# A macaron layer with neighbourhood and dilated attention: the layout in DRAM of queries, keys and values, and the order in which they are read back

## The chip, the core and the metric

The kernel runs on one core of one Trainium2 chip. The time is the device time of one execution in microseconds (us); of the kernel before there are three runs, of which the median counts. The engines are called as in the profile: PE is TensorE (matmuls; PEld its weight loads), DVE VectorE, ACT ScalarE, POOL GpSimd, SP SyncE. SP computes nothing here; it only issues transfers. POOL computes a little and issues transfers too. All of an engine's instructions, its transfers among them, go out in the order in which they stand: one that waits holds all behind it.

## What is computed

One layer on x of 1024 tokens by 1024 numbers, in fp32. Each of its three parts normalises its input and its output (RMSNorm) and adds the result to x:

```python
h = swiglu(rmsnorm(x, g1), w_gate, w_up, w_down);  x = x + 0.5 * rmsnorm(h, g2)
h = rmsnorm(x, mix_pre_g)
q, k, v = split(h @ w_qkv)                         # 16 heads of 64
o_na  = neighbourhood_attention(q[:8], k[:8], v[:8], rel_bias)
o_dil = dilated_mixture_attention(q[8:], k[8:], v[8:], t5_bias)
mixed = concat(rmsnorm(o_na), rmsnorm(o_dil)) @ w_out;  x = x + rmsnorm(mixed, g3)
h = swiglu(rmsnorm(x, g4), ...);                   x = x + 0.5 * rmsnorm(h, g5)
```

The tokens form a grid of 16 rows by 64 columns. In neighbourhood attention a token sees 8 rows by 16 columns about it, with a learned bias. In dilated attention it sees three windows (every token, every 4th, every 16th) with a bias by distance, and the three results are merged by their softmax denominators.

## The kernel before, in words

**Precision.** Each fp32 operand is split into a high part (fp32r) and a low part, the remainder. A product of two matrices is three matmuls (lines 262 to 264).

**Stages.** First the FFN, then a stage for values, queries and keys (the normalised rows and the weights are cut in quarters, and seven products of sums of quarters take the place of eight), then attention, the output projection and the second FFN. Values, queries, keys and bias tables go through DRAM: a stage writes them, and attention reads them per head in another layout.

**What is written.** The values are kept per token as a row of 4 x 130 numbers: 4 pairs of heads, each with 2 x 64 numbers and two ones, which give the softmax sums. `c.v[0]` holds those of neighbourhood, `c.v[1]` those of dilated attention, in the order of tokens. They are written by POOL, 128 tokens to a transfer, at line 1427 (`vearly`, half of the neighbourhood values) and line 1448 (`vrows`, the others). `QKPairs.put` (lines 817 to 845) writes queries and keys of a pair of heads, half of the tokens at a time: ACT casts the high part (line 834), DVE makes the low part (line 835), and POOL writes each part with a transfer of its own into `c.qk[p][kind]`, of shape [2 parts, 128, 1024]. Line 840 writes neighbourhood queries, which are permuted into strips; line 843 dilated keys, permuted by token modulo 4; line 845 the rest in plain order. The tile `e` that holds both parts has three buffers while queries and keys are made; ACT waits at line 829 or 834 if none is free.

**What is read.** The heads come in pairs: 4 to 7 (dilated) first, then 0 to 3 (neighbourhood). `load_head` (line 1334) asks for a head's data, and for a pair's values ahead of its first head:
- its stack (`load_stack`, lines 848 to 858), by POOL. The tile `st` has 128 partitions. Slot 0 holds the query: its high part on partitions 0 to 63, its low part on 64 to 127. Slots 1 and 2 hold the high and the low part of the key, on both halves alike. One matmul with slot 1 and one with slot 2 (lines 981 and 1093) then give all four products of parts. The stack is read with four transfers, a query and a key transfer for each half. The tile is fp32r, its source fp32, so the transfers cast. There are two buffers, and for every third dilated head one in another pool.
- the values. `dil_values` (line 900) loads those of pair 4 when its first head is loaded, and those of pairs 5 to 7 in one piece with pair 5: `va` for the near windows in twelve transfers of 32 partitions, `vb` for the far ones in four of 128. `na_v` (line 1058) loads a neighbourhood pair's `vs` in 16 transfers of 8 partitions. All are issued by SP.
- its bias table, by SP: `DilPair.bias` (line 935, tile `g`, two transfers) or `na_bias` (line 1066, tile `nb`). POOL then copies or adds to the table (lines 863 and 1537) before DVE uses it.

The order in `load_head` is: stack, then values if the head is its pair's first, then the table. Each SP transfer also waits for the one issued eight before it.

**A head.** It is a row of units. Each unit makes scores (line 981 or 1093), takes the row maxima together with the bias (DVE, line 881), exponentials (ACT, line 886), transposes them (line 892), copies the result (line 897) and multiplies with the values (line 993 or 1106); the steps of several units overlap, and the scores run ahead of the value products by four units. A dilated head has 8 units: `part` 1 (far windows, `vb`) and `part` 0 (near windows, `va`); only the very first head begins with `part` 0. A neighbourhood head has 8 units too. When the dilated heads have been merged, matmuls of the output projection are spread among the units that are left, at an even rate. The order of PE, DVE and ACT in this stage is that in which the code is written; SP and POOL are ordered by the scheduling layer, by dependence and readiness.

Of the kernel before, what the change touches and what calls it, by code (L numbers as in the profile page):

```python
# [19 lines left out]
P, T = 128, 512  # L20
# [776 lines left out]
class QKPairs:  # L797
# [19 lines left out]
    def put(self, b, kind, h, x):  # L817
# [18 lines left out]
        d = c.qk[p][kind]  # L836
        for j in range(2):
            if strip:
                dst = d[j].rearrange("p (s r c) -> p s (r c)", s=8, r=16)[:, :, h * 64:h * 64 + 64]
                nc.gpsimd.dma_start(dst, e[:, j].bitcast(F32).rearrange("p (s x) -> p s x", s=8))  # L840
            elif kind and p >= NP:
                dst = d[j].rearrange("p (c h t) -> p h c t", c=4, h=2)[:, h]
                nc.gpsimd.dma_start(dst, parts[j].bitcast(F32))
            else:
                nc.gpsimd.dma_start(d[j, :, h * T:(h + 1) * T], e[:, j].bitcast(F32))


def load_stack(c, p, hd, pool):

    nc = c.nc  # L850
    st = pool.tile([P, 3, SEQ], F32R, tag="st", name="st", bufs=2 if pool is c.stk else 1)
    rows = slice(hd * 64, hd * 64 + 64)
    q, k = c.qk[p]
    for u in range(2):
        dst = slice(u * 64, u * 64 + 64)
        nc.gpsimd.dma_start(st[dst, 0, :], q[u, rows, :])
        nc.gpsimd.dma_start(st[dst, 1:3, :], k[:, rows, :].rearrange("j p n -> p j n"))
    return st
# [41 lines left out]
def dil_values(c, pool, p, n):  # L900

    w, row = n * VW, 16 * VW
    va = pool.tile([P, 11, w], F32, tag="va", name="va", bufs=1)
    vb = pool.tile([P, 4, 2, w], F32, tag="vb", name="vb", bufs=1)
    v = c.v[1][:, (p - NP) * VW:(p - NP) * VW + w]
    for ci in range(4):
        to = va[ci * 32:ci * 32 + 32]
        for u0, m, t0 in ((0, 7, 16), (7, 2, 0), (9, 2, 192)):
            c.nc.sync.dma_start(to[:, u0:u0 + m], bass.AP(tensor=v.tensor, offset=v.offset + ci * 4 * VW + t0 * row,
                                                          ap=[[row, 32], [32 * row, m], [1, w]]))  # L910
    for ci in range(4):
        c.nc.sync.dma_start(vb[:, ci], v.rearrange("(j i c) f -> c i j f", j=2, c=4)[ci])
    return va, vb


class DilPair:
# [17 lines left out]

    def bias(self, hd, third):
        c, nc = self.c, self.c.nc
        g = (c.op if third else c.gp).tile([P, 3, 384], F32, tag="g", name="g", bufs=1 if third else 2)
        for i in range(2):
            nc.sync.dma_start(g[:, 2 - i], c.gab[i][2 * self.pi + hd, :, 127:511])
        return g  # L940
# [10 lines left out]
    def unit(self, hd, st, q, g, part, quad, un, po):  # L951
# [5 lines left out]
        def scores():  # L957
# [4 lines left out]
            for j in range(2):  # L962
# [8 lines left out]
                else:  # L971
# [5 lines left out]
                    ex = sj.rearrange("p (c u t) -> p u c t", c=4, u=2)  # L977
                    pj = pb[:, j].rearrange("p (u c t) -> p u c t", u=2, c=4)
# [79 lines left out]
def na_v(c, p):  # L1058
    vs = c.vp.tile([P, 8, VW], F32, tag="v" + "ab"[p % 2], name="vs")
    src = c.v[0][:, p * VW:(p + 1) * VW].rearrange("(r s c) f -> r c s f", r=16, s=8)  # L1060
    for r in range(16):
        c.nc.sync.dma_start(vs[r * 8:r * 8 + 8], src[r])
    return vs

# [106 lines left out]
def layer(tc, a, out):  # L1171
    nc = tc.nc
    c = Ctx(tc)
    with ExitStack() as ctx:
# [20 lines left out]
        c.qk = [[c.dr.tile([2, P, SEQ], F32, name=f"qk{p}_{k}") for k in range(2)] for p in range(8)]  # L1195
# [138 lines left out]
        def load_head():  # L1334
# [23 lines left out]
        with ExitStack() as order:  # L1358
# [64 lines left out]
            def vearly(p, t, ps):  # L1423
# [3 lines left out]
                nc.gpsimd.dma_start(vs1[t] if p == 0 else c.v[0][t * P:(t + 1) * P, :], v)  # L1427
# [18 lines left out]
            def vrows(t, h):  # L1446
                for g in range(t < 4, 2):
                    nc.gpsimd.dma_start(c.v[g][t * P:(t + 1) * P, :], h[:, g])
# [227 lines left out]
```

## Time and profile before

| | us |
|---|---|
| three runs, median (lowest, highest) | 1956.05 (1955.32, 1956.93) |
| the profiled execution, its own time | 1954.08 |
| its span in the trace | 1952.3 |
| TensorE busy in the span | 1867.3 |
| VectorE, ScalarE, GpSimd busy | 1313.9, 804.1, 325.4 |
| TensorE busy from 900 to 1000 us / 1000 to 1100 / 1100 to 1200 | 89.16 / 99.33 / 87.42 |

How to read the rows that follow. A row of a stretch gives its start and end, its length, then for each engine the busy us and, in brackets, the number of instructions; then the granted clock of TensorE (1.00 is full), the share of time in which the 16 DMA engines were busy, and GB/s. A row of the timeline gives start, length, engine, line, operation, output and inputs, how many are merged, and in square brackets the idle time before it and what ended it. A row of waits gives the waiting engine and line, what it waited for, the total in us, how often, and the longest. An engine named with a q (SPq) is its issuing side. "DMA st<-qk" is a transfer into tile `st` from tensor `qk`.

### The profile page before, as it was taken

To read this page: it belongs to the slowest core of one execution; us is meant where nothing else is said; L and a number is where in the kernel's file an instruction comes from. 1 tells how busy PE (TensorE), PEld (TensorE's weight loads), DVE (VectorE), ACT (ScalarE), POOL (GpSimd) and SP (SyncE) were. 2 spreads that over 40 slices of the span, in tenths; PEclk is the share of its full clock that TensorE was granted. 3 is DMA by queue.
4 is the path that set the end of the run, shared out by engine and by line. 5 is a ranking of instruction groups with operands and counts; after the bars stand their busy time and mean duration, and the time that the engine had idled before them with its cause. 6 is when DMAs were issued, how large, how long until landed. Compare 5 with 4: busy or idle time off the path is not lost.

```text
span 1952.3 us, 25216 instructions
## 1 busy us (share of the span) xinstructions
PE 1867.3 (96%) x9044; PEld 1559.5 (80%) x9044; DVE 1313.9 (67%) x2205; ACT 804.1 (41%) x1287; POOL 325.4 (17%) x536
## 2 busy tenths in 40 slices
PE   5999999999999989999899889998999999999997
PEld 4788888888888868778799887776888888888886
DVE  5778776765656766567456556676788777754557
ACT  4522333333534445233567655454222333344332
POOL 2101111111000123233443310121011111110000
PEclk8999999999999999999899989998999999999999
DMA  6555565546976667768997961574556665476663
GB/s 241 214 172 178 178 236 194 211 161 237 324 250 207 244 216 251 242 217 228 281 205 135 199 125 44 183 276 160 168 183 208 233 216 194 153 265 225 197 231 131
DMA packets 165246, 400.97 MB, mean 205 GB/s; under 512 B 18737, under 2 KB 35297, under 8 KB 165121
## 3 DMA queue, kind: packets, MB, share of 16 engines
q1 hardware_dynamic: 113616, 224.63, 36.4%
q0 software_dynamic: 50640, 172.64, 27.8%
q10 hardware_dynamic: 864, 2.10, 0.3%
q8 instruction: 71, 1.16, 0.2%
q14 instruction: 55, 0.44, 0.1%
HBM read 274.84 MB, written 129.50 MB: 207 GB/s over the span
## 4 chain that ended last, share of the span: by engine, by line
PE 78%; DMA 9%; DVE 6%; issue 5%; ACT 1%; POOL 1%; SPq 0%; DVEq 0%; POOLq 0%; ACTq 0%
PE mmp L264 16%; PE mmp L262 16%; PE mmp L263 16%; PE accp L263 7%; PE accp L264 7%; PE accp L262 7%; PE po L993 2%; PE ptp L892 2%; PE trp L170 1%; PE sp L981 1%; DMA vs<-v 1%; PE po L1106 1%; DMA g<-gab 1%; DMA x<-x 1%; DMA va<-v 1%
## 5 line engine op out<-in xcount | busy, mean ns | idle before, releaser
L262 PE MATMUL mmp<-x,whi 128*128 128x512 f32 (+1 forms) x1464 | 579.7, 396 | 7.6 <-ACT whi L355 3.6
L264 PE MATMUL mmp<-x,wlo 128*128 128x512 f32 (+1 forms) x1464 | 574.9, 393 | 1.0 <-DVE wlo L356 1.0
L263 PE MATMUL mmp<-x,whi 128*128 128x512 f32 (+1 forms) x1464 | 574.5, 392 | 0.6 <-DVE x L172 0.5
L262 PEld LDWEIGHTS mmp<-x,whi 128*128 128x128 f32 x1464 | 277.9, 190 | 67.5 <-ACT whi L355 4.2
L264 PEld LDWEIGHTS mmp<-x,wlo 128*128 128x128 f32 x1464 | 277.8, 190 | 62.2 <-DVE wlo L356 1.9
L263 PEld LDWEIGHTS mmp<-x,whi 128*128 128x128 f32 x1464 | 278.1, 190 | 59.8 <-DVE x L172 1.5
L613 DVE TENSOR_TENSOR pw<-praw,pw 128x1024 fp32r<-128x1024 f32 (+1 forms) x182 | 199.3, 1138 | 122.8 <-ACT pw L612 122.4
L612 ACT CAST pw<-praw 128x1024 fp32r<-128x1024 f32 (+1 forms) x182 | 169.5, 983 | 206.0 <-PE accp L264 167.7
L355 ACT CAST whi<-wraw 128x1024 fp32r<-128x1024 f32 x129 | 135.2, 1050 | 249.4 <-PE mmp L263 216.7
L262 PE MATMUL accp<-pw 128*128 128x512 f32 x600 | 234.4, 391 | 0.6 <-DVE hb L684 0.6
L264 PE MATMUL accp<-pw 128*128 128x512 f32 x600 | 233.5, 389 | 0.0
L263 PE MATMUL accp<-pw 128*128 128x512 f32 x600 | 233.4, 389 | 0.0
L356 DVE TENSOR_TENSOR wlo<-wraw,whi 128x1024 fp32r<-128x1024 f32 x129 | 157.6, 1225 | 24.9 <-ACT whi L355 24.8
L262 PEld LDWEIGHTS accp<-pw 128*128 128x128 f32 x600 | 112.6, 188 | 24.2 <-issue 1.0
L264 PEld LDWEIGHTS accp<-pw 128*128 128x128 f32 x600 | 112.6, 188 | 23.5
L263 PEld LDWEIGHTS accp<-pw 128*128 128x128 f32 x600 | 112.7, 188 | 23.3
L560 POOL DMA_DIRECT2D g<-sg x44 | 23.9, 542 | 472.3 <-DVE sg L553 285.6
L374 ACT COPY s<-mmp 128x512 f32<-128x512 f32 x52 | 30.5, 587 | 147.9 <-PE mmp L264 146.3
L518 DVE TENSOR_TENSOR c<-mmp,u 128x512 f32<-128x512 f32 x52 | 35.9, 691 | 82.5 <-PE mmp L264 82.2
L172 DVE TENSOR_TENSOR x<-trp,x 128x512 fp32r<-128x512 f32 x84 | 57.2, 687 | 35.0 <-ACT x L171 35.0
L355 ACT CAST whi<-traw 128x512 fp32r<-128x512 f32 x52 | 32.3, 621 | 116.9 <-PE mmp L263 58.4
L443 DVE TENSOR_TENSOR wraw<-wraw 128x1024 f32<-128x1024 f32 x52 | 63.6, 1224 | 23.6 <-DMA wraw<-in_wqk_dram 12.5
(230 smaller groups left out, 2739.2 us busy)
## 6 DMA issues: line engine op xcount, KB each, us to landing
praw<-g SPq DMA_DIRECT2D x70, 512.0 KB
wraw<-in_wg_dram SPq DMA_DIRECT2D x44, 512.0 KB
wraw<-in_wu_dram SPq DMA_DIRECT2D x44, 512.0 KB
tr<-in_wd_dram SPq DMA_DIRECT2D x44, 512.0 KB
g<-sg POOLq DMA_DIRECT2D x88, 256.0 KB, 3.9
ts<-tr POOLq DMA_DIRECT2D x22, 1024.0 KB, 4.7
praw<-ts SPq DMA_DIRECT2D x88, 256.0 KB
praw<-in_wd_dram SPq DMA_DIRECT2D x66, 256.0 KB
```

Of the source, the lines that this page charges most:

```text
L172: nc.vector.tensor_sub(lo, ps, hi.bitcast(F32))
L262: nc.tensor.matmul(out, ahi, bhi, start=start, stop=False, skip_group_check=go_on)
L263: nc.tensor.matmul(out, ahi, blo, start=False, stop=False, skip_group_check=go_on)
L264: nc.tensor.matmul(out, alo, bhi, start=False, stop=stop, skip_group_check=go_on)
L355: nc.scalar.copy(hi, raw)
L356: nc.vector.tensor_sub(lo, raw, hi.bitcast(F32))
L443: nc.vector.tensor_sub(r[:, 0:2], r[:, 1:3], r[:, 0:2])
L518: nc.vector.tensor_add(c21, d, u2)
L612: nc.scalar.copy(w[side][:, 0, :m], raw[:, :m])
L613: nc.vector.tensor_sub(w[side][:, 1, :m], raw[:, :m], w[side][:, 0, :m].bitcast(F32))
L892: c.nc.tensor.transpose(self.tps[:, j, :], self.probs[:, j * P:(j + 1) * P], c.ident)
L993: nc.tensor.matmul(po[0][:, un * 2 + j], u.pt[:, 2 * j + t, :], rhs, start=t == 0, stop=t == 1)
```

## The change

Six edits. PE, DVE and ACT keep their instructions and their order, save for the permutation in 5:

1. `c.qk` has the shape [128, 2 parts, 1024]: the parts of a row alternate. `put` writes both parts of plain rows with one transfer; permuted ones still take two.
2. `load_stack` reads the stack in two transfers over 128 partitions. High and low part of the query alternate by partition, and each partition gets both key parts of its row as one run of 8 KB. The destination is written as fp32, so nothing is cast.
3. The values in DRAM stand in the order of use: `put_values` writes them, with two transfers for every 128 tokens where there was one. `na_v` reads a pair's with one transfer, `dil_values` reads `va` with three transfers of 128 partitions.
4. `vb` is read with eight transfers (four residues, two halves) where there were four.
5. The exponentials of `part` 0 are written in another permutation, so that the keys agree with the new order of the values.
6. In `load_head` a head's table is asked for ahead of its pair's values; `dil_bias` is the former method `bias`.

```diff
@@ QKPairs.put
+        if not strip and not (kind and p >= NP):
+            nc.gpsimd.dma_start(d[:, :, h * T:(h + 1) * T], e.bitcast(F32))
+            return
         for j in range(2):
             if strip:
-                dst = d[j].rearrange("p (s r c) -> p s (r c)", s=8, r=16)[:, :, h * 64:h * 64 + 64]
+                dst = d[:, j].rearrange("p (s r c) -> p s (r c)", s=8, r=16)[:, :, h * 64:h * 64 + 64]
...
-            else:
-                nc.gpsimd.dma_start(d[j, :, h * T:(h + 1) * T], e[:, j].bitcast(F32))
@@ load_stack
-    rows = slice(hd * 64, hd * 64 + 64)
-    q, k = c.qk[p]
-    for u in range(2):
-        dst = slice(u * 64, u * 64 + 64)
-        nc.gpsimd.dma_start(st[dst, 0, :], q[u, rows, :])
-        nc.gpsimd.dma_start(st[dst, 1:3, :], k[:, rows, :].rearrange("j p n -> p j n"))
+    q, k = [bass.AP(tensor=x.tensor, offset=x.offset + hd * 64 * 2 * SEQ, ap=ap)
+            for x, ap in zip(c.qk[p], ([[SEQ, P], [1, SEQ]], [[2 * SEQ, 64], [0, 2], [1, 2 * SEQ]]))]
+    nc.gpsimd.dma_start(st[:, 0, :].bitcast(F32), q)
+    nc.gpsimd.dma_start(st[:, 1:3, :].rearrange("p j n -> p (j n)").bitcast(F32), k)
@@ dil_values
-    for ci in range(4):
-        to = va[ci * 32:ci * 32 + 32]
-        for u0, m, t0 in ((0, 7, 16), (7, 2, 0), (9, 2, 192)):
-            c.nc.sync.dma_start(to[:, u0:u0 + m], bass.AP(tensor=v.tensor, offset=v.offset + ci * 4 * VW + t0 * row,
-                                                          ap=[[row, 32], [32 * row, m], [1, w]]))
-    for ci in range(4):
-        c.nc.sync.dma_start(vb[:, ci], v.rearrange("(j i c) f -> c i j f", j=2, c=4)[ci])
+    for u0, m, m0 in ((0, 7, 1), (7, 2, 0), (9, 2, 12)):
+        c.nc.sync.dma_start(va[:, u0:u0 + m], bass.AP(tensor=v.tensor, offset=at + m0 * row,
+                                                      ap=[[4 * VW, P], [2 * row, m], [1, w]]))
+    for ci in range(4):
+        for j in range(2):
+            c.nc.sync.dma_start(vb[:, ci, j], bass.AP(tensor=v.tensor, offset=at + 8 * j * row + ci * 16 * 4 * VW,
+                                                      ap=[[row, 8], [4 * VW, 16], [1, w]]))
@@ DilPair.unit, scores
-                    ex = sj.rearrange("p (c u t) -> p u c t", c=4, u=2)
-                    pj = pb[:, j].rearrange("p (u c t) -> p u c t", u=2, c=4)
+                    ex = sj.rearrange("p (c m i) -> p m c i", c=4, m=4)
+                    pj = pb[:, j].rearrange("p (m c i) -> p m c i", m=4, c=4)
@@ na_v
-    src = c.v[0][:, p * VW:(p + 1) * VW].rearrange("(r s c) f -> r c s f", r=16, s=8)
-    for r in range(16):
-        c.nc.sync.dma_start(vs[r * 8:r * 8 + 8], src[r])
+    c.nc.sync.dma_start(vs, c.v[0][:, p * VW:(p + 1) * VW].rearrange("(s p) f -> p s f", s=8))
@@ new
+def put_values(c, g, t, x):
+    for i in range(2):
+        if g:
+            dst = c.v[1].rearrange("(m c i) f -> m i c f", c=4, i=16)[2 * t + i]
+        else:
+            dst = c.v[0].rearrange("(s r c) f -> r s c f", s=8, r=16)[2 * t + i]
+        c.nc.gpsimd.dma_start(dst, x[i * 64:i * 64 + 64])
@@ load_head
             st = load_stack(c, p, hd, c.op if third else c.stk)
+            g = dil_bias(c, p - NP, hd, third) if p >= NP else na_bias(c, p, hd)
             if hd == 0:
                 pairs[p] = ...
-            loaded.append((pairs[p], st, pairs[p].bias(hd, third) if p >= NP else na_bias(c, p, hd)))
+            loaded.append((pairs[p], st, g))
```

How the order moves. SP, where pair 5's first head is loaded, before (`va`, `vb` are the values of pairs 5 to 7, `gab` the bias tables):

```order
L909 DMA va<-v_88 32x7x390
L909 DMA va<-v_88 32x2x390 x2
L912 DMA vb<-v_88 128x2x390 x4
L939 DMA g<-gab_68 128x384
L939 DMA g<-gab_69 128x384
```

SP at the same place now:

```order
L918 DMA g<-gab_68 128x384
L918 DMA g<-gab_69 128x384
L906 DMA va<-v_88 128x7x390
L906 DMA va<-v_88 128x2x390 x2
L910 DMA vb<-v_88 128x1x390 x8
L1493 DMA gd<-in_na_out_g_dram 128x512
```

The head's two tables stand ahead of the values, and the gains `gd`, which stood among the `va` transfers, behind them.

SP in the neighbourhood part, before (`vs` are a pair's values, `nb` tables, `wraw` weights of the output projection):

```order
L1062 DMA vs<-v_87 8x8x130 x6
L103 DMA wraw<-in_wo_dram 128x1024 x2
L1062 DMA vs<-v_87 8x8x130 x10
L1068 DMA nb<-nb 128x384 x2
L1062 DMA vs<-v_87 8x8x130 x3
```

SP at the same place now, each transfer with its number:

```order
L1059 DMA vs_9511<-v0_87 128x8x130
L103 DMA wraw_9494<-in_wo_dram 128x1024
L103 DMA wraw_9496<-in_wo_dram 128x1024
L1075 DMA nb_9509<-nb_70 128x384
L1075 DMA nb_9671<-nb_70 128x384
L1059 DMA vs_9857<-v0_87 128x8x130
```

Between two tables stands one transfer of values where there were up to sixteen.

POOL where neighbourhood stacks are loaded, before; the first two rows are the second half of a stack, and the same two rows for its first half stand ahead of them:

```order
L856 DMA st<-qk_0_71 64x1024
L857 DMA st<-qk_1_72 64x2x1024
L1047 TENSOR_TENSOR obn<-obn,w 128x8x2x64
L1048 TENSOR_TENSOR oa<-oa,w 128x16x64
L1537 TENSOR_TENSOR nb<-nb,cmask 128x384
```

POOL at the same place now:

```order
L855 DMA st<-qk_0_71 128x1024
L856 DMA st<-qk_1_72 128x1x2048
L1046 TENSOR_TENSOR obn<-obn,w 128x8x2x64
L1047 TENSOR_TENSOR oa<-oa,w 128x16x64
L1548 TENSOR_TENSOR nb<-nb,cmask 128x384
```

Two transfers of full height stand where four of half height stood; what follows them is the same.

More of the change, by code (lines that the diff above doesn't have):

```diff
@@ L900, in dil_values, with dil_bias @@
 def dil_values(c, pool, p, n):
-    w, row = n * VW, 16 * VW
+    w, row = n * VW, 64 * 4 * VW
     va = pool.tile([P, 11, w], F32, tag="va", name="va", bufs=1)
     vb = pool.tile([P, 4, 2, w], F32, tag="vb", name="vb", bufs=1)
-    v = c.v[1][:, (p - NP) * VW:(p - NP) * VW + w]
+    v, at = c.v[1], c.v[1].offset + (p - NP) * VW
+    for u0, m, m0 in ((0, 7, 1), (7, 2, 0), (9, 2, 12)):
+        c.nc.sync.dma_start(va[:, u0:u0 + m], bass.AP(tensor=v.tensor, offset=at + m0 * row,
+                                                      ap=[[4 * VW, P], [2 * row, m], [1, w]]))
     for ci in range(4):
-        to = va[ci * 32:ci * 32 + 32]
-        for u0, m, t0 in ((0, 7, 16), (7, 2, 0), (9, 2, 192)):
-            c.nc.sync.dma_start(to[:, u0:u0 + m], bass.AP(tensor=v.tensor, offset=v.offset + ci * 4 * VW + t0 * row,
-                                                          ap=[[row, 32], [32 * row, m], [1, w]]))
-    for ci in range(4):
-        c.nc.sync.dma_start(vb[:, ci], v.rearrange("(j i c) f -> c i j f", j=2, c=4)[ci])
-    return va, vb
+        for j in range(2):
+            c.nc.sync.dma_start(vb[:, ci, j], bass.AP(tensor=v.tensor, offset=at + 8 * j * row + ci * 16 * 4 * VW,
+                                                      ap=[[row, 8], [4 * VW, 16], [1, w]]))
+    return va, vb
+def dil_bias(c, pi, hd, third):
+    g = (c.op if third else c.gp).tile([P, 3, 384], F32, tag="g", name="g", bufs=1 if third else 2)
+    for i in range(2):
+        c.nc.sync.dma_start(g[:, 2 - i], c.gab[i][2 * pi + hd, :, 127:511])
+    return g
 class DilPair:
@@ L933, in outputs @@
         self.ob = c.op.tile([P, 8, RW], F32, tag="ob", name="ob")
[L935 to L940, printed above, removed]
     def head(self, hd, st, q, g, late, parts=(1, 0)):
@@ L1059, in na_v @@
     vs = c.vp.tile([P, 8, VW], F32, tag="v" + "ab"[p % 2], name="vs")
-    src = c.v[0][:, p * VW:(p + 1) * VW].rearrange("(r s c) f -> r c s f", r=16, s=8)
-    for r in range(16):
-        c.nc.sync.dma_start(vs[r * 8:r * 8 + 8], src[r])
-    return vs
+    c.nc.sync.dma_start(vs, c.v[0][:, p * VW:(p + 1) * VW].rearrange("(s p) f -> p s f", s=8))
+    return vs
+def put_values(c, g, t, x):
+    for i in range(2):
+        if g:
+            dst = c.v[1].rearrange("(m c i) f -> m i c f", c=4, i=16)[2 * t + i]
+        else:
+            dst = c.v[0].rearrange("(s r c) f -> r s c f", s=8, r=16)[2 * t + i]
+        c.nc.gpsimd.dma_start(dst, x[i * 64:i * 64 + 64])
 def na_bias(c, p, hd):
@@ L1194, in layer @@
         c.nb = c.dr.tile([8, P, 16, 24], F32, name="nb")
-        c.qk = [[c.dr.tile([2, P, SEQ], F32, name=f"qk{p}_{k}") for k in range(2)] for p in range(8)]
+        c.qk = [[c.dr.tile([P, 2, SEQ], F32, name=f"qk{p}_{k}") for k in range(2)] for p in range(8)]
         c.v = [c.dr.tile([SEQ, 4 * VW], F32, name=f"v{g}") for g in range(2)]
@@ L1426, in vearly @@
                 nc.scalar.copy(by_head(v), ps.rearrange("p (h f) -> p h f", f=64))
-                nc.gpsimd.dma_start(vs1[t] if p == 0 else c.v[0][t * P:(t + 1) * P, :], v)
+                if p == 0:
+                    nc.gpsimd.dma_start(vs1[t], v)
+                else:
+                    put_values(c, 0, t, v)
             vp = Passes(c, 4, op, getv, vearly)
```

5 lines of the change are left out of this document (2 added, 3 removed).

## The prediction

> **What bounds the kernel now.** I read the page's first two parts, then the busy time by stretches over the whole span, then the waits of TensorE, then, for each of its waits, the rows of the engine and the queue behind it, and last the DMA queues.
>
> The page's head, and the first row of its busy table:
>
> ```profile
> span 1952.3 us, 25216 instructions
> ```
>
> ```profile
> PE 1867.3 (96%) x9044; PEld 1559.5 (80%) x9044; DVE 1313.9 (67%) x2205; ACT 804.1 (41%) x1287; POOL 325.4 (17%) x536
> ```
>
> TensorE is the bound almost everywhere; 85 us of the span are idle. What the change can win is idle time of TensorE, and the time in which it runs at half the granted clock after a stall. The attention stage, which begins in the first of the next rows, has three such places. The busy time by stretches there (TensorE first; the granted clock is the number before the DMA share):
>
> ```profile
> 940.00:945.00 5.00, 2.83 (x18) 2.23 (x16) 1.23 (x2) 0.28 (x1) 3.65 (x7) 1.00 1.05 332
> 945.00:950.00 5.00, 1.22 (x4) 0.93 (x4) 3.96 (x17) 4.94 (x6) 3.47 (x5) 0.59 1.12 271
> 950.00:955.00 5.00, 4.66 (x22) 4.50 (x23) 0.88 (x6) 4.85 (x12) 1.14 (x2) 0.50 1.32 234
> 955.00:960.00 5.00, 5.00 (x42) 5.00 (x41) 2.82 (x11) 2.30 (x5) 1.89 (x3) 0.89 1.08 345
> 980.00:985.00 5.00, 0.88 (x8) 0.65 (x6) 2.20 (x12) 1.73 (x5) 3.17 (x3) 0.84 0.85 301
> 985.00:990.00 5.00, 5.00 (x25) 5.00 (x25) 1.67 (x7) 1.84 (x5) 2.73 (x5) 0.50 1.00 183
> 1115.00:1120.00 5.00, 0.00 (x0) 0.00 (x1) 0.00 (x0) 0.00 (x0) 0.66 (x2) 0.66 1.28 194
> 1120.00:1125.00 5.00, 4.97 (x23) 4.90 (x23) 0.00 (x0) 1.10 (x3) 0.00 (x0) 0.50 1.17 183
> 1125.00:1130.00 5.00, 1.35 (x5) 0.85 (x4) 0.14 (x1) 0.00 (x0) 0.14 (x1) 0.50 0.47 98
> 1130.00:1135.00 5.00, 3.75 (x15) 3.55 (x16) 5.00 (x13) 4.34 (x12) 2.25 (x2) 0.50 0.00 0
> 1135.00:1140.00 5.00, 5.00 (x22) 4.74 (x22) 3.31 (x9) 4.09 (x7) 0.00 (x0) 0.50 0.11 30
> ```
>
> Each stall drags a stretch at clock 0.50 behind it, where 5 us hold 22 to 25 matmuls, not the 42 of the fourth row. TensorE's waits from 936 to 1145 us (total, times, longest):
>
> ```profile
> PE sp L1093 <- DMA st<-qk: 7.4, 3, 6.0
> PE sp L981 <- DVE sa L881: 4.9, 1, 4.9
> PE po L1106 <- ACT pt L897: 4.9, 1, 4.9
> PE po L993 <- ACT pt L897: 4.1, 1, 4.1
> PE ptp L892 <- ACT pb L886: 1.0, 1, 1.0
> ```
>
> I call the places first start (943 to 957 us: 4.9 + 1.0 idle), second pair (980 to 990: 4.1) and neighbourhood part (1100 to 1140: 7.4 + 4.9). The waits for ACT and DVE are links of chains that begin with transfers. For the first start, the row of ACT, and the two of POOL behind which transfers stood:
>
> ```profile
> 944.72 0.63 ACT L829 ACTIVATE qk<-c 128x512 f32<-128x512 f32 x1 [4.91 <-DMA qk<-qk]
> ```
>
> ```profile
> 934.77 0.85 POOL L863 COPY g<-g 128x384 f32<-128x384 f32 x1 [7.00 <-DMA g<-gab]
> ```
>
> ```profile
> 981.83 0.85 POOL L863 COPY g<-g 128x384 f32<-128x384 f32 x1 [11.62 <-DMA g<-gab]
> ```
>
> POOL waits 7.00 us for the first head's bias table and meanwhile doesn't issue the query and key writes queued behind it; ACT's last query evacuation waits 4.91 us for the buffer that such a write still reads; DVE's first row maxima stand behind that, and TensorE behind them. At 981.83 it is the table of pair 5's first head. Why the tables are late, SP's issues say (start, length, line):
>
> ```profile
> 920.10 6.86 SPq L939 DMA_DIRECT2D g<-gab  x4
> 932.79 3.18 SPq L909 DMA_DIRECT2D va<-v  x7
> ...
> 949.68 8.14 SPq L912 DMA_DIRECT2D vb<-v  x4
> 958.52 8.43 SPq L939 DMA_DIRECT2D g<-gab  x4
> ...
> 1104.00 15.18 SPq L1062 DMA_DIRECT2D vs<-v  x10
> 1120.35 0.82 SPq L1068 DMA_DIRECT2D nb<-nb  x2
> ```
>
> The first tables stand behind 16 value transfers, pair 5's behind 16 more, and the neighbourhood table whose lack is behind the 4.9 us after 1125 behind ten small value transfers that held SP for 15.18 us. The 7.4 us are the head's own stack.
>
> **The stacks (first term).** A neighbourhood head's stack is asked for when TensorE has left that buffer, one head earlier:
>
> ```profile
> 1091.40 0.55 POOL L856 DMA_DIRECT2D st<-qk  x1 [4.30 <-PE sp L1093]
> ```
>
> ```profile
> 1101.71 0.57 POOL L856 DMA_DIRECT2D st<-qk  x1 [1.58 <-PE sp L1093]
> ```
>
> So a head takes 10.3 us, and a stack must land within that. The one asked for at 1101.71 was not there at 1115: the row of 1115 to 1120 has TensorE at 0.00. The DMA queues (packets, MB, share of 16 engines), first from 1065 to 1140 us, where POOL's queue (q0) carries only stacks (1.57 MB each, 3 x 128 x 1024 numbers of 4 bytes, so five), then from 600 to 700 us, where it carries 128-partition transfers:
>
> ```profile
> q0 software_dynamic: 2294, 8.03, 63.2%
> q1 hardware_dynamic: 3763, 3.80, 26.0%
> ```
>
> ```profile
> q0 software_dynamic: 2231, 8.10, 22.7%
> ```
>
> The same bytes in as many packets: 0.632 x 75 = 47.4 us of all 16 engines for half-height transfers, 0.227 x 100 = 22.7 us for full-height ones. Per stack that is 9.5 us against 4.5; with SP's share (0.26 x 75 / 5 = 3.9 us a head) the engines are asked for 13.4 us in a 10.3 us period now, and 8.4 after. The waits for stacks should go: 7.4 us. Bounds: nothing gained, if the narrow destination isn't what slows them, and all. I take all, since the two rows differ in little but height (the cast to fp32r goes too). The load must then finish in 10.3 us with its latency; I keep 1 us of wait.
>
> [...]
>
> **The order of SP (second term).** The neighbourhood values become one transfer a pair instead of 16, so SP isn't held: the 4.9 us go. The clock: TensorE's busy time between 1115 and 1140 us is 0 + 4.97 + 1.35 + 3.75 + 5.00 = 15.1 us at 0.50, so 7.5 us lost to it go as well. Neighbourhood part: 7.4 + 4.9 + 7.5 = 19.8 us. What is late next there is nothing that the profile shows: the engines' order is unchanged, the output matmuls that fill the stage are a fixed amount, and the waits of TensorE listed above name no other cause.
>
> Second pair: the tables of pair 5 now stand ahead of the 11 value transfers: 4.1 us go, and half of the 5.00 us busy at 0.50, 2.5. Sum 6.6. It holds if the pair's `vb`, which `part` 1 uses first, lands in time. TensorE first uses it here:
>
> ```profile
> 991.03 1.00 PE L993 MATMUL po<-vb,pt 128*128 128x65 f32 x8
> ```
>
> Less 6.6 and the 2.8 us of the next paragraph, that is 981.6 us; the transfers are asked for from 932.79 on, as now.
>
> First start: the table is asked for before the values, lands before POOL reaches its copy, and the query write goes out some 3 us earlier. ACT's L829 then waits for its input, made by this row of DVE:
>
> ```profile
> 941.19 0.69 DVE L518 TENSOR_TENSOR c<-mmp,u 128x512 f32<-128x512 f32 x1 [0.65 <-PE mmp L264]
> ```
>
> 941.9 in place of 944.72: 2.8 us, and everything behind on ACT and DVE moves with it. The rest stays, for ACT still has its other casts, the query copy and a table load to do before the first exponentials. Bounds 0 and, with all idle and the clock (5.9 + 0.41 x 1.22 + 0.50 x 4.66 + 0.11 x 5.00 = 9.3), 9.3.
>
> **The `vb` transfers.** Four become eight per load, each read as 8 rows of 16. [...] No row of before has their shape; the nearest is that of `vs<-v`, also 8 outermost: ten of 32.5 KB in 15.18 us. At that rate, 21 KB/us, eight of 195 KB take 73 us. The other bound is the old `vb`, asked for from 949.68 and landed before the table behind it was used at 981.83. I take the old one, as the ten small transfers ran beside a stack and held only 64 packets each: no cost.
>
> **What is written.** Key and query writes to plain rows become one issue instead of two, 16 in all; value writes become two instead of one, 16 in all. On POOL these cancel. The value writes that matter are the first four:
>
> ```profile
> 703.93 0.55 POOL L1427 DMA_DIRECT2D v<-vt  x1
> ```
>
> ```profile
> 709.50 0.11 POOL L1425 MEMSET vt<- 128x8 f32 x1 [3.12 <-DMA v<-vt]
> ```
>
> Each adds 0.55 us ahead of a reload of the normalised rows that TensorE's transposes need there, and the buffer comes free later. Between 0 and 4 x 0.55 = 2.2; I take 0.6, one of them. The other twelve come in one run late in the value stage, with nothing but key writes behind them on POOL: between 0 and 12 x 0.55 = 6.6; I take 0, as those keys are read only in the attention stage. The permuted exponentials cost nothing: those with 32-long runs and those in plain order take the same.
>
> ```profile
> L886 ACT ACTIVATE s<-s,ob 128x256 f32<-128x256 f32 x64 | 29.0, 504 | 9.5 <-DVE ob L881 9.5
> L886 ACT ACTIVATE pb<-s,sa 128x256 f32<-128x256 f32 x64 | 28.9, 503 | 3.3 <-DVE sa L881 3.0
> ```
>
> **Sum.** 19.8 + 6.6 + 2.8 - 1.0 - 0.6 = 27.6 us. The profiled execution took 1954.08 us (span 1952.3), 1.97 below the median 1956.05; it would take 1926.5, and the median 1928.5.
>
> **The rivals.**
> *Half-height isn't the cause.* The stacks stay slow (because of the cast, or of DRAM). Then 4.9, half of the 7.5, 6.6 and 2.8 are won: 18.0, so 1938. For it: those rows don't part height from cast. Against: fewer SP transfers would speed the stacks anyway. 14%.
> *Values in place of tables.* Pair 5 waits for `vb` as long as it now waits for its table: 27.6 - 6.6 = 21.0, so 1935. 8%.
> *Values far too late (slower).* If `vb` goes at the 21 KB/us of `vs<-v`, the first pair's eight (520 KB, 24 us) hold SP until about 936 (from 912 on, an estimate: the old 16 were issued by 920.10). Behind them come 2.2 MB of `va` (9 us at the 234 GB/s of 950 to 955), then the 73 us: 936 + 9 + 73 = 1018, 36 us after 981.6, with 3 us of slow clock behind. 39 lost against 27.6 won: 1968. It is a loss from a landing at about 1006 on. Against it: the old `vb` of the same 1.6 MB, asked for at 949.68, was in by 981.83, under 32.2 us, beside stacks. 4%.
> The change doing nothing would need the stacks slow and both tables late; the orders exclude the latter.
>
> **How the numbers follow.** Forecast 74%, with a range of its own of 1919 (first start wholly gone, 6.5 more, and the 1.6 of costs nil, with a few us for the clock's steps) to 1936 (a third of the neighbourhood term stays). With 1938, 1935 and a little above, the range is 1919 to 1942; the slow case and the tails are left out. About 0.2%, 3.9 us, is what a measurement here tells from no change. Faster by more: forecast and the two smaller gains, less a little, 0.94; within 0.02; slower 0.04.
>
> **What would show it.** Right: POOL's queue from the first neighbourhood head on takes about half the engine time per MB; no wait of `sp` for `st<-qk`; no clock of 0.50 after 960 us within the stage; POOL's copy of `g` not waiting. Wrong: a wait of POOL or TensorE for stacks as long as now (second case), idle time before `po<-vb` at the second pair (third and fourth), or TensorE idle near 705 to 720 us by more than now.

## The result, and the profile after

The changed kernel takes 1926.66 us (median of 4 runs, 1922.9 to 1928.74), the kernel before 1955.68 beside it: a ratio of 0.9853, 95% interval 0.9836 to 0.9869, so 29 us faster. The forecast was 1928.5. The profiled execution took 1925.22 us, with this head and busy table:

```profile
span 1923.4 us, 25041 instructions
...
PE 1856.8 (97%) x9044; PEld 1551.0 (81%) x9044; DVE 1313.8 (68%) x2205; ACT 802.5 (42%) x1287; POOL 311.0 (16%) x504
```

TensorE does the same matmuls, 9044, in the same order. It is busy 10.5 us less, since it does fewer of them at the low clock (mean granted clock 0.988 against 0.980), and idle 18.4 us less (66.6 against 85.0). In stretches about the three places of the prediction (TensorE first, the granted clock before the DMA share):

```profile
946.00:951.00 5.00, 1.45 (x9) 0.93 (x8) 4.32 (x18) 4.97 (x7) 3.96 (x6) 0.94 1.03 374
951.00:956.00 5.00, 5.00 (x35) 4.95 (x34) 1.55 (x8) 4.55 (x12) 2.95 (x3) 0.72 1.03 380
...
975.00:980.00 5.00, 5.00 (x47) 5.00 (x46) 3.36 (x14) 4.12 (x10) 0.87 (x2) 1.00 0.85 282
980.00:985.00 5.00, 5.00 (x48) 5.00 (x46) 2.33 (x12) 3.69 (x9) 3.98 (x5) 1.00 0.90 238
...
1103.00:1108.00 5.00, 5.00 (x42) 4.87 (x41) 4.81 (x14) 4.64 (x14) 1.23 (x2) 1.00 0.90 328
1108.00:1113.00 5.00, 4.52 (x35) 3.85 (x33) 4.43 (x9) 5.00 (x10) 0.27 (x1) 1.00 0.60 148
1113.00:1118.00 5.00, 3.69 (x20) 3.70 (x21) 2.71 (x11) 1.97 (x5) 1.17 (x2) 0.66 0.94 325
```

The second pair (975 to 985) has no idle time and no low clock left. The first start still has both, less of each. In the neighbourhood part the 25 us from 1115 to 1140, at clock 0.66 and then 0.50, have become one stretch of 5 us at 0.66, at a place that had no wait before. TensorE's waits from 930 to 1145 us say what stands at each place now:

```profile
PE sp L980 <- DVE sa L880: 2.3, 1, 2.3
PE ptp L891 <- DVE pt L896: 1.6, 1, 1.6
PE ptp L891 <- ACT pb L885: 1.3, 1, 1.3
```

No wait for `st<-qk` (7.4 before) is in that list any more. The 1.6 us are those near 1113. There DVE's order puts two splits of output weights (L111) ahead of its copy of transposed probabilities; the first two rows are the splits, the last the copy that TensorE waits for:

```profile
1110.25 1.23 DVE L111 TENSOR_TENSOR wlo<-wraw,whi 128x1024 fp32r<-128x1024 f32 x1 [0.41 <-ACT whi L110]
...
1112.08 1.22 DVE L111 TENSOR_TENSOR wlo<-wraw,whi 128x1024 fp32r<-128x1024 f32 x1
...
1113.70 0.55 DVE L896 COPY pt<-ptp 128x384 f32<-128x384 f32 x1
```

Before, the same splits stood at 1137.67 and 1139.80, where TensorE's granted clock was 0.50 (1135 to 1140) and DVE kept up with it.

The DMA queues from 1060 to 1130 us, and what the stacks took from issue to landing:

```profile
q0 software_dynamic: 1728, 9.44, 36.6%
q1 hardware_dynamic: 4704, 5.15, 23.6%
...
st<-qk POOLq DMA_DIRECT2D x6, 1024.0 KB, 7.2
st<-qk POOLq DMA_DIRECT2D x6, 512.0 KB, 4.5
```

POOL's queue takes 0.366 x 70 / 9.44 = 2.71 us of all 16 engines per MB; before it was 0.632 x 75 / 8.03 = 5.90. A stack of 1.57 MB costs 4.3 us (the prediction had 4.5). The row of 600 to 700 us, from which that was taken, gives 0.227 x 100 / 8.10 = 2.80 for other transfers of full height.

TensorE's order being the same, one and the same matmul can be found in both traces, and the difference of its starts says what was won up to it. The marks, by their start before: 851.84 us (in the stage of values and keys), 961.34 (behind the first start), 990.36 (behind the second pair), 1092.24 and 1140.02 (ends of the neighbourhood part's disturbed stretch), 1145.30, and the last matmul, 1941.21. The table has the difference to before over each stretch, in us, minus for faster, rounded so that a row adds up. Each row is one traced execution, set against the one of before. The experiments of the next section stand in it too, save the one that alters TensorE's order (query and weights); "after, again" is a second execution of the changed kernel.

| | to 852 | first start, to 961 | second pair, to 990 | to 1092 | neighbourhood, to 1140 | to 1145 | rest | all |
|---|---|---|---|---|---|---|---|---|
| after | +3.3 | -5.0 | -7.0 | -1.3 | -19.6 | +2.9 | -2.1 | -28.8 |
| after, again | +4.1 | -4.8 | -7.0 | -1.3 | -19.2 | +1.6 | -3.0 | -29.6 |
| tables first | +1.0 | +0.4 | -7.0 | +0.3 | -7.4 | +1.0 | -3.2 | -14.9 |
| stacks only | +2.3 | -5.0 | -1.2 | -1.1 | -18.8 | +2.9 | -4.0 | -24.9 |
| values only | +2.6 | +0.1 | -3.1 | -0.5 | -16.6 | +2.6 | -1.8 | -16.7 |
| half height | +3.0 | +0.9 | -7.0 | +5.7 | -13.6 | +1.5 | -4.3 | -13.8 |
| cast kept | +3.1 | -4.8 | -7.0 | -1.3 | -19.6 | +2.9 | -3.9 | -30.6 |
| tables behind | -1.0 | -4.6 | -7.0 | -1.3 | -19.6 | +2.9 | +0.7 | -29.9 |
| early query | +1.5 | -7.2 | -7.0 | -1.3 | -19.6 | +1.6 | -1.7 | -33.7 |
| splits on POOL | -0.9 | -3.6 | -7.0 | -1.3 | -19.6 | +0.7 | -1.8 | -33.5 |
| both of these | +4.2 | -7.0 | -7.1 | -1.3 | -19.5 | +0.7 | -3.2 | -33.2 |

The columns of the second pair, to 1092 and of the neighbourhood part repeat to a few tenths where the cause is the same. The first start does so less well (3.6 us won with the splits on POOL, which should not touch it, 4.6 to 5.0 otherwise), and the first column and the rest vary by some us between executions.

### The profile page after: what moved, and what is told of

Same layout as the page of the kernel before. It is cut to its first block, busy times and chain, and to the rows that moved or that the text cites. A ratio compares the mean times of both kernels' runs of the same rounds, so it can differ in the third digit from the quotient of the medians.

```text
span 1923.4 us, 25041 instructions
## 1 busy us (share of the span) xinstructions
PE 1856.8 (97%) x9044; PEld 1551.0 (81%) x9044; DVE 1313.8 (68%) x2205; ACT 802.5 (42%) x1287; POOL 311.0 (16%) x504
## 4 chain that ended last, share of the span: by engine, by line
PE 59%; issue 27%; DVE 5%; DMA 5%; POOL 3%; ACT 1%; SPq 0%; POOLq 0%; DVEq 0%; ACTq 0%
PE mmp L264 10%; PE mmp L263 10%; PE mmp L262 10%; PE accp L262 5%; PE accp L263 5%; PE accp L264 5%; PE po L992 3%; PE ptp L891 2%; PE sp L980 2%; PE po L1113 2%; PE trp L170 1%; POOL g L579 1%; PE sp L1100 1%; DMA wraw<-in_wqk_dram 1%; DMA x<-x 1%
## 5 line engine op out<-in xcount | busy, mean ns | idle before, releaser
L356 DVE TENSOR_TENSOR wlo<-wraw,whi 128x1024 fp32r<-128x1024 f32 x129 | 157.7, 1224 | 24.9 <-ACT whi L355 24.6
L518 DVE TENSOR_TENSOR c<-mmp,u 128x512 f32<-128x512 f32 x52 | 35.9, 691 | 84.7 <-PE mmp L264 84.3
L172 DVE TENSOR_TENSOR x<-trp,x 128x512 fp32r<-128x512 f32 x84 | 57.3, 687 | 36.4 <-ACT x L171 36.4
```

The lines of the kernel that those rows point to most:

```text
L172: nc.vector.tensor_sub(lo, ps, hi.bitcast(F32))
L356: nc.vector.tensor_sub(lo, raw, hi.bitcast(F32))
```

## The experiments

The theory: there are three gains, each from its own edit. Stacks of full height cost the DMA engines half (4.5 us against 9.5, by the prediction's rows); fewer value transfers free SP; tables that stand ahead come in time. The main rival: half height is not the cause (the cast, or the short runs, slow the stacks).

**Tables first**: the kernel before with edit 6 alone.

```diff
             st = load_stack(c, p, hd, c.op if third else c.stk)
+            g = dil_bias(c, p - NP, hd, third) if p >= NP else na_bias(c, p, hd)
             if hd == 0:
```

> The kernel before with edit 6 alone: a head's table is asked for ahead of its pair's values. Theory (three separate gains): the 4.1 us of the second pair and its stretch of low clock go, about 7 us, some 1 to 3 us of the first start as well, and nothing in the neighbourhood part, where TensorE still waits about 7 us for stacks and 5 us for the table: 1946 to 1949 us. Rival (the tables were late because the DMA engines were full of half-height stacks, and the order hardly matters): under 3 us, 1953 or more, with POOL's copy of the table of pair 5 still waiting 8 us or more.

Measured: 1939.32 us, ratio 0.9932 (0.991 to 0.9955), 13 us won, more than expected. The second pair gains its 7.0 us as said, the first start nothing. What was overlooked is that `na_bias` stands in the same line: the neighbourhood tables too now go ahead of their pair's values. SP's issues:

```profile
1098.72 0.33 SPq L1075 DMA_DIRECT2D nb<-nb  x1
1099.10 15.60 SPq L1069 DMA_DIRECT2D vs<-v  x10
```

SP is held as long as before (15.60 us), but the table is no longer behind it, and the wait of 4.9 us with its clock is gone; the stack wait stays:

```profile
PE sp L1100 <- DMA st<-qk: 7.9, 3, 5.5
```

**Stacks only**: the kernel before with edits 1 and 2.

```diff
-    for u in range(2):
-        dst = slice(u * 64, u * 64 + 64)
-        nc.gpsimd.dma_start(st[dst, 0, :], q[u, rows, :])
-        nc.gpsimd.dma_start(st[dst, 1:3, :], k[:, rows, :].rearrange("j p n -> p j n"))
+    nc.gpsimd.dma_start(st[:, 0, :].bitcast(F32), q)
+    nc.gpsimd.dma_start(st[:, 1:3, :].rearrange("p j n -> p (j n)").bitcast(F32), k)
```

> The kernel before with edits 1 and 2 alone: the parts of queries and keys alternate in DRAM, and a stack is read with two uncast transfers of full height. Theory: POOL's queue takes about 2.8 us of all engines per MB in the neighbourhood part, where it took 5.9, and TensorE's 7.4 us of waits for stacks go with some 3 us of low clock; the 4.9 us behind the held-up table stay, or shrink because the small value transfers share the engines with less. 1940 to 1946 us. Rival (the small value transfers that hold SP are the cause of both waits): TensorE still idles 8 us or more between 1100 and 1140 us, 1950 or more. If the loss of 2.9 us in the stage of values and keys is due to the merged writes of queries and keys, it shows here.

Measured: 1927.72 us, ratio 0.9877 (0.9848 to 0.9906), 24 us won, far more than expected: these two edits by themselves bring most of the whole. POOL's queue, and the two long runs of neighbourhood values on SP:

```profile
q0 software_dynamic: 1728, 9.44, 39.4%
```

```profile
1094.80 6.96 SPq L1061 DMA_DIRECT2D vs<-v  x13
...
1119.52 10.58 SPq L1061 DMA_DIRECT2D vs<-v  x13
```

The engine time is 0.394 x 70 / 9.44 = 2.92 us per MB, and thirteen small transfers hold SP for 6.96 and 10.58 us where ten took 15.18 before. Each waits for the landing of the one issued eight before it (before, SP waited 7.8 us for `vs` and 7.2 us for two `wraw` transfers so, from 1085 to 1130 us), and with nothing but the stacks altered the issues are through sooner. SP's queue as a whole takes 0.228 x 70 / 5.13 = 3.1 us of all 16 engines per MB from 1060 to 1130 us, where it took 0.287 x 70 / 3.75 = 5.4 before, in a somewhat different mix of transfers. So the wait for the neighbourhood table goes with the stacks alone. At the second pair a wait of 2.9 us for POOL's copy of the table stays (the table has only 1.2 of 7.0 won there).

**Values only**: the kernel before with edits 3, 4 and 5; the tables stay behind.

```diff
-    for r in range(16):
-        c.nc.sync.dma_start(vs[r * 8:r * 8 + 8], src[r])
+    c.nc.sync.dma_start(vs, c.v[0][:, p * VW:(p + 1) * VW].rearrange("(s p) f -> p s f", s=8))
```

> The kernel before with edits 3, 4 and 5 alone: values in DRAM in the order of use, read with few transfers, tables behind them. Theory: SP is not held in the neighbourhood part, so the 4.9 us and some 2.5 us of low clock go, and with fewer small packets in the way the stack wait shrinks a little but stays; at the second pair the table still comes late. 1945 to 1950 us. Rival (the value layout gives nothing by itself): 1953 or more. If the loss of 2.9 us in the stage of values and keys is due to the value writes in two transfers, TensorE shows it here, at 808 to 850 us, and not in the run with the stacks alone.

Measured: 1940.96 us, ratio 0.993 (0.9915 to 0.9946), 14 us won, again more than expected. With POOL's queue as busy as ever,

```profile
q0 software_dynamic: 2577, 9.03, 72.3%
```

the stack wait still shrank to less than half:

```profile
PE sp L981 <- POOL q L863: 3.2, 2, 2.5
PE sp L1101 <- DMA st<-qk: 3.0, 3, 2.1
```

That SP's 16 small transfers a pair no longer run beside a stack is a likely reason, but not a shown one: SP's queue takes 30.4% of the engines here and 28.7% before, in the same window. The first row was 0.4 before. Its longest wait, 2.5 us, ends at the mark at 961 and leaves a mean granted clock of 0.85 over the 23 us from 957 to 980 (1.00 before and after), so that only 3.1 of the second pair's 7.0 us are won.

**Half height**: the changed kernel with each of its two stack transfers cut in two of 64 partitions; bytes, runs and the missing cast as in the change.

```diff
-    nc.gpsimd.dma_start(st[:, 0, :].bitcast(F32), q)
-    nc.gpsimd.dma_start(st[:, 1:3, :].rearrange("p j n -> p (j n)").bitcast(F32), k)
+    for u in range(2):
+        for t, x in ((st[:, 0, :], q), (st[:, 1:3, :].rearrange("p j n -> p (j n)"), k)):
...
+            nc.gpsimd.dma_start(t[u * 64:u * 64 + 64].bitcast(F32), src)
```

> The changed kernel with its stack read as four transfers of 64 partitions, the same rows in the same runs of bytes and still without a cast. Theory (height is what counts): POOL's queue takes some 5 us or more of all engines per MB in the neighbourhood part, a stack takes about 9 us of the engines, and TensorE waits for stacks again, though less than before as SP's small transfers are gone: 3 to 8 us with the clock, 1930 to 1935 us. Rival (the cast, or the short runs, were what slowed the stacks): engine time per MB stays near 2.8 us, no wait of the scores for a stack, 1927 us as with the change.

Measured: 1942.31 us, ratio 0.9944 (0.9927 to 0.9961): 18 us slower than the change by the ratios, more than the 3 to 8 expected. The rival falls.

```profile
q0 software_dynamic: 1868, 9.23, 61.1%
```

```profile
PE sp L983 <- DVE sa L883: 6.0, 1, 6.0
PE sp L1103 <- DMA st<-qk: 3.2, 2, 2.7
```

0.611 x 70 / 9.23 = 4.63 us per MB against 2.71, with nothing altered but the height and, with it, the number of transfers. The number is not the reason: the two traces have the same 768 packets of 8192 bytes in POOL's queue from 1060 to 1130 us, and the median one takes 309 ns at full height and 636 at half. The two profiled executions are 15.0 us apart, and the table shows where: about 6 at the first start, 7 from 990 to 1092 (a wait of 2.3 us, then a granted clock of 0.55 and 0.59 from 1008 to 1016) and 6 in the neighbourhood part, less some 4 elsewhere. At the first start ACT waits for its write buffer again:

```profile
948.00 0.63 ACT L829 ACTIVATE qk<-c 128x512 f32<-128x512 f32 x1 [4.75 <-DMA qk<-qk]
```

**After, again**, the changed kernel beside the next three.

> The changed kernel, unaltered, timed beside the three that follow: 1927 us, 27 to 30 below the kernel before. It also tells whether the 2.9 us that it lost at 808 to 850 us, in the stage of values and keys, belong to the change: the run with the tables alone, which changes nothing in that stage, had a drop of the clock at 811 us as well. Theory (chance from run to run): they come and go. Rival (the value writes): the same 2 to 3 us again.

Measured: 1923.98 us, ratio 0.9852 (0.983 to 0.9873), as in the first place. The loss ahead of 852 us was there again, 4.1. That alone would speak for the rival; the run with the tables behind says more.

**Cast kept**: the changed kernel with an fp32r destination, so that the full-height transfers cast.

```diff
-    nc.gpsimd.dma_start(st[:, 0, :].bitcast(F32), q)
-    nc.gpsimd.dma_start(st[:, 1:3, :].rearrange("p j n -> p (j n)").bitcast(F32), k)
+    nc.gpsimd.dma_start(st[:, 0, :], q)
+    nc.gpsimd.dma_start(st[:, 1:3, :].rearrange("p j n -> p (j n)"), k)
```

> The changed kernel with the destination of the stack left fp32r, so that its two full-height transfers cast as the four of the kernel before did. Theory (height is what counts, the cast costs nothing): POOL's queue takes 2.8 to 3 us of all engines per MB in the neighbourhood part, no wait of the scores for a stack, the time of the changed kernel within 2 us. Rival (the cast costs): 4 us per MB or more, waits for stacks of some us, 1930 us or more.

Measured: 1924.2 us, ratio 0.985 (0.9828 to 0.9873), the time of the change; no wait for a stack.

```profile
q0 software_dynamic: 1728, 9.44, 39.0%
```

2.89 us per MB against 2.71: the cast costs next to nothing here, and the kernel doesn't feel it.

**Tables behind**: the changed kernel with edit 6 undone.

```diff
-            g = dil_bias(c, p - NP, hd, third) if p >= NP else na_bias(c, p, hd)
             if hd == 0:
                 pairs[p] = ...
-            loaded.append((pairs[p], st, g))
+            loaded.append((pairs[p], st, dil_bias(c, p - NP, hd, third) if p >= NP else na_bias(c, p, hd)))
```

> The changed kernel with edit 6 undone: the tables stand behind the values of their pair again. Theory (with fast stacks and few transfers of values the neighbourhood part no longer needs the order; the second pair still does): the neighbourhood part as with the change, at the second pair 2 to 4 us of wait and a stretch of low clock, 3 to 6 us slower than the change, 1930 to 1933 us. Rival (with fast stacks the order is worth nothing): within 1 us of the change. By the prediction's own term it would be 6.6 us and part of the first start, 8 us.

Measured: 1925.7 us, ratio 0.9865 (0.9843 to 0.9887), which the interval doesn't part from the change; the trace gives the same 7.0 us at the second pair and 4.6 at the first start. The rival held: beside the other edits the order of the tables is worth nothing that can be measured. POOL's copies wait longer for their tables, and still come in time, for TensorE is busy without a gap from 957 to 992 (35.00 us of 35):

```profile
929.77 0.87 POOL L862 COPY g<-g 128x384 f32<-128x384 f32 x1 [9.02 <-DMA g<-gab]
...
966.12 0.89 POOL L862 COPY g<-g 128x384 f32<-128x384 f32 x1 [14.65 <-DMA g<-gab]
```

This run also bears on the loss ahead of 852 us. It holds all edits that act there, and has none: full clock in both stretches,

```profile
805.00:815.00 10.00, 8.04 (x36) 6.32 (x35) 6.25 (x8) 0.83 (x1) 4.41 (x7) 1.00 0.86 235
845.00:855.00 10.00, 10.00 (x46) 8.23 (x45) 7.18 (x9) 5.18 (x6) 3.72 (x5) 1.00 0.62 213
```

while the run with the tables alone, which changes nothing ahead of 900 us, has the drop at the first of them:

```profile
805.00:815.00 10.00, 7.91 (x28) 6.06 (x27) 5.92 (x8) 0.27 (x1) 3.49 (x7) 0.83 0.94 253
```

So most of that loss hangs on the execution. Whether a part of it belongs to the change stays open: the eight rows of the table with all edits that act there run from -1.0 to +4.2, with a mean of 2.2, and without those edits there are only two traces, before (0) and the tables alone (+1.0).

**Query and weights**: the changed kernel, the first head's query copy on POOL, and the splits of output weights two units later.

```diff
-            c.behind(lambda: qs.append(q_by_residue(c, nc.scalar.copy, loaded[0][1])), ACT)
+            c.behind(lambda: qs.append(q_by_residue(c, nc.gpsimd.tensor_copy, loaded[0][1])), POOL)
...
-both(n0.scale(), n1.squares(every)) + weights
+both(n0.scale(), n1.squares(every)) + [lambda: None] * 2 + weights
```

> The changed kernel with two alterations meant to take out what is left. First, the first head's query copy by residue goes from ACT, where it takes 2.04 us ahead of the first exponentials, to POOL. Second, the two splits of output weights (DVE, 1.23 us each), which with the change fall ahead of DVE's copy of transposed probabilities and make TensorE wait 1.6 us near 1112 us with some 3.4 us of low clock behind it, stand two units later. Theory (both waits have the cause named): the wait for DVE's maxima at the first start shrinks from 2.3 us to about 0.5 and what it drags, 2 to 3 us; the wait at 1112 goes with its clock, 3 us; 4 to 6 us faster than the change, 1921 to 1923 us. Rival (another link comes out late at the same place, such as DVE's casts at the start or the next DVE copy at 1112): within 1 us of the change.

Measured: 1928.46 us, ratio 0.9879 (0.9859 to 0.9899), some 5 us slower than the change beside it (the fastest of its five executions took 1927.69 us, the slowest of the change's four 1925.43). The wait for ACT's `pb` went, and a longer one came: the copy on POOL ends too late for the scores that need it.

```profile
PE sp L980 <- POOL q L862: 3.7, 1, 3.7
PE sp L980 <- DVE sa L880: 2.3, 1, 2.3
```

Of the wait of 1.6 us for DVE's copy near 1112 only 0.3 was left; but from 1145 to 1250 us TensorE is busy 98.35 us, where it was 100.36 with the change, and by 1260 us nothing of the gain remained.

**Early query**: the changed kernel with the same copy on ACT, one evacuation earlier.

```diff
-            c.behind(lambda: qs.append(q_by_residue(c, nc.scalar.copy, loaded[0][1])), ACT)
+            acts = [i for i in nc.cur_bb.bb.instructions if i.engine == ACT]
+            with c.tc.issue_after(acts[-5]):
+                qs.append(q_by_residue(c, nc.scalar.copy, loaded[0][1]))
```

> The changed kernel with the first head's query copy by residue still on ACT, but one evacuation earlier, ahead of ACT's L829, where ACT idles 2.15 us for DVE. Theory (the first exponentials come late because ACT copies 2.04 us ahead of them, and the copy must be done by 951 us, when the run with the copy on POOL waited 3.7 us for it): TensorE's wait for ACT's pb, 1.3 us, goes, the wait for DVE's maxima of 2.3 us stays, 1 to 3 us faster than the change with the clock, 1921 to 1923 us where the change measured 1924. Rival (DVE, not ACT, is last at the first start): within 1 us, the wait for pb replaced by a longer one for DVE.

**Splits on POOL**: the changed kernel with four of the weight splits on POOL.

```diff
-        nc.vector.tensor_sub(lo, raw, hi.bitcast(F32))
+        (nc.gpsimd if c.left else nc.vector).tensor_sub(lo, raw, hi.bitcast(F32))
```

> The changed kernel with the splits of output weights made during the neighbourhood heads (four, L111) on POOL, which is 17% busy, and not on DVE. Theory (DVE in its order makes TensorE wait 1.6 us near 1112 us): that wait and 1.5 to 3.4 us of low clock go, 3 us faster than the change. Rival one (what is gained there is given back, as in the run that put the splits two units later: the output matmuls then wait elsewhere, and by 1300 us nothing is left): within 1 us. Rival two (POOL's subtraction is slow and the output matmuls wait for it): slower by 2 us or more, with a wait of accp for POOL.

**Both of these.**

> The two alterations of the runs beside it together: the earlier query copy on ACT and the splits on POOL. They stand at different places (945 to 950 us and 1110 to 1118 us), so by the theory their gains add: 4 to 6 us faster than the change, 1918 to 1920 us. Rival: under 2 us, because what is won ahead is waited for later.

Measured: 1921.71 us (ratio 0.9851, 0.9831 to 0.987), 1924.47 (0.9856, 0.9835 to 0.9876) and 1918.92 (0.984, 0.9818 to 0.9862), where the change had 0.9852. In whole time none is parted from the change; in the trace each does its part. ACT's copy now stands in what was idle time, and costs L829 behind it 0.23 us:

```profile
940.95 2.02 ACT L862 CAST q<-st 128x1024 fp32r<-128x1024 f32 x1
943.20 0.63 ACT L829 ACTIVATE qk<-c 128x512 f32<-128x512 f32 x1 [0.23 <-ACT q L862]
```

The first start is then 7.2 and 7.0 us faster than before, not 4.8 to 5.0, and the granted clock is 1.00 from 943 to 957 us in both (0.88 with the change). With the splits on POOL the loss up to 1145 us is 0.7, not 1.6 to 2.9, with 0.9 us of waits for DVE's L172 in its place. The sum of both, 3 to 4 us, is near the difference of the ratios (0.0012, 2.3 us), but the intervals don't part it from zero.

## Why the prediction came out as it did

**The stacks** (7.4 us, and their share of the clock) were right in mechanism. The rate fell from 5.90 to 2.71 us per MB, no score waits for a stack, and the residual wait of 1 us that the sum kept did not come. The run at half height shows the height to be the cause, and the run with the cast that the cast is not, at full height. Between 4.63 (half height, no cast, longer runs) and 5.60 to 5.74 (half height as before, in the runs with values or tables alone) there is another 1 us per MB, from the cast, the runs of 4 KB or the traffic beside them; these were not parted.

The prediction's second case, in which the stacks stay slow at full height, doesn't hold: the same bytes cost 1.7 times the engine time in halves (4.63 against 2.71 us per MB), and 18 us of the kernel. Why a packet of 8192 bytes takes 636 ns there against 309, no run shows.

**The neighbourhood part** was forecast at 18.8 us with that residual and measured 19.6 (19.2 in the second execution). The step that failed is the division: 4.9 us to the value transfers that hold SP, 7.4 to the stacks, as if each edit had its own. Alone, the tables win 7.4 there, the stacks 18.8 and the values 16.6; the whole is 19.6. SP was held for 15.18 us because its transfers landed slowly beside the stacks, as the run with the stacks alone shows (6.96 and 10.58 us there), and the stacks came late in part because of the values, whose change alone takes the stack wait from 7.4 to 3.0 us. Either side relieved frees the other. Also wrong was that nothing would be late next: 2.9 us (1.6 in the second execution) are given back up to 1145, so that the part wins 16.7 (17.6) in all.

**The second pair** was forecast at 6.6 and measured 7.0, but its named cause, the tables' order, is not needed: with them behind the values the same 7.0 are won. Alone it suffices, as the run of it shows. In the changed kernel, fast stacks and few value transfers bring the table in time in either order.

**The first start** was forecast at 2.8 and measured 5.0; the 2.8 are idle time of TensorE, the rest clock (0.63 on average from 943 to 957 us before, 0.88 now). The effect on ACT came out as forecast. DVE's L518, which makes the input of ACT's L829, shows that the trace is shifted by 3.05 us here (944.24 against 941.19). Less that shift, POOL's copy of the table starts 5.0 us earlier than before, the query writes go out 3.1 us earlier (933.04, 936.11 before), and L829 starts at 941.97 in place of 944.72:

```profile
944.24 0.69 DVE L518 TENSOR_TENSOR c<-mmp,u 128x512 f32<-128x512 f32 x1 [0.66 <-PE mmp L264]
```

```profile
932.79 0.88 POOL L862 COPY g<-g 128x384 f32<-128x384 f32 x1 [7.78 <-DMA g<-gab]
...
936.09 1.77 POOL L843 DMA_DIRECT2D qk<-qk  x2 [1.83 <-ACT qk L834]
...
955.39 0.89 POOL L862 COPY g<-g 128x384 f32<-128x384 f32 x1
```

```profile
945.02 0.64 ACT L829 ACTIVATE qk<-c 128x512 f32<-128x512 f32 x1 [2.15 <-DVE c L518]
```

The step that failed is the cause, edit 6. Of the prediction's four signs this one did not come: POOL's copy still waits for a table, 7.78 us. It is the second head's table (before the change too), which the first pair's values still precede:

```profile
910.61 4.64 SPq L906 DMA_DIRECT2D va<-v  x3
915.29 6.77 SPq L910 DMA_DIRECT2D vb<-v  x8
922.10 14.54 SPq L918 DMA_DIRECT2D g<-gab  x4
...
941.85 21.86 SPq L910 DMA_DIRECT2D vb<-v  x8
```

(The fourth row is for the rivals below. The copy for pair 5's first head, the one at 955.39, waits for nothing any more.) Less the shift of each run, the copy starts 4.2 us earlier than before with the stacks alone and 3.8 with the tables behind, but 1.1 with the tables alone, 1.8 to 2.8 with the values alone (the shift changes there by 1.0), and 0.6 later at half height, where ACT's wait for its write buffer is back (4.75 us). That the table lands sooner because stacks of full height leave the engines more room fits these numbers; it is argued, not shown by itself.

ACT's wait is not the whole of it. With the tables alone and the values alone it is gone as well, and TensorE's first wait, 4.9 us before, is shorter (the tables alone, then the values alone):

```profile
944.21 0.63 ACT L829 ACTIVATE qk<-c 128x512 f32<-128x512 f32 x1 [2.15 <-DVE c L518]
```

```profile
PE sp L988 <- DVE sa L881: 2.9, 1, 2.9
```

```profile
PE sp L981 <- DVE sa L881: 3.0, 1, 3.0
```

Yet neither run wins anything in the table's column: TensorE then waits 1.1 and 2.5 us for POOL's copy of a query (0.4 before), which stands in POOL's order behind the transfers of half-height stacks, and other time goes to the clock (0.68 and 0.76 on average from 943 to 957 us) and, with the values alone, to a wait of 0.7 us for DVE's `v`. With the stacks alone all 5.0 are won, at half height none. So it is the full height of the stacks on which the gain of the first start hangs.

**What was not in the sum.** The 2.9 and 1.6 us given back up to 1145: TensorE, at a granted clock of 1.00 (1108 to 1113 us) where it had 0.50, meets DVE's splits of 1.23 and 1.22 us. The 3.3 and 4.1 us ahead of 852, which for the most part come and go. The 1.3 between 990 and 1092 and the 2 to 3 us behind 1145, won. These nearly cancel: 3.3 + 2.9 - 1.3 - 2.1 = 2.8 lost, against 2.2 + 0.4 + 0.8 = 3.4 more won than forecast at the three places, and the 0.6 put down for value writes, which can't be told from the scatter ahead of 852 (the run with the tables behind has them all and is 1.0 us ahead there). That 27.6 us were forecast and 28.8 came is thus in part luck.

**The rivals.** The first (half height isn't the cause) is refuted; its 18.0 us for all but the stacks was too much, for the change with half height won 11. The values that take the place of tables, and the values far too late, did not come. The eight `vb` transfers of pairs 5 to 7 were issued from 941.85 to 963.71 (the fourth row of SP above), and the first use waits for nothing:

```profile
982.35 1.00 PE L992 MATMUL po<-vb,pt 128*128 128x65 f32 x8
```

## What to carry to other kernels

When several transfers share the engines, price them by engine time per MB from the queue's share, not by their own waits: here the slow stacks were also paid for by SP's queue (5.4 us per MB beside them, 3.1 in a somewhat different mix with nothing but the stacks altered) and by SP itself (held 15.18 us by ten value transfers, then 6.96 and 10.58 by thirteen). Read into all partitions at once (2.71 against 4.63 us per MB here). And when three waits have a common cause, don't add the edits' gains: here the ratios of each alone add up to 51 us, and 29 is what there was.

## What the runs showed that was not expected

In these traces waits that differ by tenths of a microsecond came with and without a drop of TensorE's clock. In the stage of values and keys one wait of its `accp` for DVE lasted 1.8 us before and 2.2 after, the one without a drop (1.00 from 805 to 815 us), the other with 0.83:

```profile
PE accp L263 <- DVE pw L613: 2.2, 1, 2.2
PE mmp L262 <- DVE c L510: 2.0, 1, 2.0
```

Waits of 2.0 us came with the drop in some executions (0.83 from 845 to 855 us after) and without it in others (1.00 there before; the run with the tables behind has two of them and 1.00 in both stretches). A drop to 0.83 over 10 us is worth 1.7 us, so a few tenths saved at such a place can win more than themselves, and no edit is to be credited with it from one execution.
